# Program order on VectorE and ScalarE in the scan of an RWKV-7 / short-convolution layer

## The chip, the core and the metric

The kernel runs on one core of a Trainium2 chip. A core has five engines with a queue of instructions each: TensorE (PE; its weight loads are shown as PEld), VectorE (DVE), ScalarE (ACT), GpSimd (POOL) and SyncE (SP). SyncE only issues transfers here; nearly all of them go through its queue, and the few that store an inverse go through POOL's. The metric is the device time of one execution in microseconds (us), the median of several runs.

## What is computed

One layer for 128 context tokens and 2048 latent tokens of width 1024. The eight heads of group A go through RWKV-7, one scan per direction; group B is a gated short convolution; both go through one output projection.

```python
def step(S, inp):
    r_t, w_t, k_t, v_t, kk_t, a_t = inp
    s_kk = jnp.einsum('bdhij,bdhj->bdhi', S, kk_t)
    S = (S * w_t[..., None, :] - s_kk[..., :, None] * (kk_t * a_t)[..., None, :]
         + v_t[..., :, None] * k_t[..., None, :])
    return S, jnp.einsum('bdhij,bdhj->bdhi', S, r_t)
s_final, ys = lax.scan(step, s0.astype(f32), xs)
y = ys[:, 0] + jnp.flip(ys[:, 1], axis=1)
...
y = ((y - mean) * lax.rsqrt(var + GN_EPS)).reshape(b, t, A_WIDTH)
y = y * lp['gn_w'].astype(f32) + lp['gn_b'].astype(f32)
...
u = jnp.concatenate([ya, yb], axis=-1) @ lp['w_out']
return x + gate * u, s_final
```

Both token groups end in an RMS norm; the final states of the context scan are returned as well.

## The kernel before

Phase 1 (lines 50 to 596) makes the normalised input, all input projections, the scan's operands (`scr_ops`, per chunk of 64 tokens), the values (`scr_vt`), the convolution's result (`scr_mixT`) and the gates, and leaves them in DRAM. The change doesn't touch it.

Phase 2 is the scan. It goes through 17 tiles of 128 tokens (`NST`), in both directions at once; a tile has two chunks. `main()` is the loop over the steps s. The names that the text uses:

- `load_units` (L692) loads the operands kb and x of one step and direction, three steps ahead (`L(d)` in the loop).
- `cross` (L708, `C(k)`) makes, for a chunk and direction of step s + 2, the products of its operands (psG). ScalarE copies a part of them to lab, VectorE masks the others to abr and x, and lab is stored to `scr_at` (L728). There are four crosses in a step, C(0) to C(3), and a `turn` (`R(k)`, psT to kbt) behind each.
- `inverse` (L744) loads lab back in another layout (ab, L749), inverts sixteen pairs of triangular blocks on POOL (L758 to L769) and stores them to `scr_zt` (L774). It is issued behind C(3), for step s + 2.
- `merge` (L825) loads the inverse (zb, L829), transposes it on VectorE (L833), and puts two halves together with two groups of small matmuls, psU and psW, and ScalarE's copies (L841, L848). It has three parts. Parts one and two of merge s + 1 run at the end of step s, part three inside step s + 1, behind the first two parts of its `step`.
- `step` (L865) is the scan itself for one chunk of both directions: psw, psy, pst, psu, with copies on ScalarE (L894, L907) and a multiplication on VectorE (L919) between. sv is the state with the next values, loaded at L863.
- `finish` (L962) normalises a finished tile y, in two parts (psv, its root and reciprocal; then psr and the products L988 to L990).
- `project` (L1014) multiplies a tile with the output weights, in pieces of six matmuls (psoc for the convolution's half, psoa for attention's). It needs the tile mr or y split in two parts, mh (ScalarE, L1010) and ml (VectorE, L1011), and a tile z, to which VectorE adds the result (L1030, L1031). `piece()` runs one piece; a step has eight. The weights of the half are split by `load_k` (L996), first for the convolution, and at step 9 for attention.

Two things set the order. A scheduler puts the instructions of each engine, and the transfers of SyncE's queue, in the order in which they come ready in its own plan of the program, and then adds the waits. `Queue` (L638) overrules it for one engine: while `held` is set, each instruction depends on the one traced before it, so that the engine keeps the order of the program. Before the change only TensorE is such a queue in phase 2.

The PSUM pools of the scan have one buffer for each tag: g (two banks, a cross), t (one bank: turn, merge, finish), w, y and s (one each: step), and two of u (projections), eight banks in all.

Of the kernel before, what the change touches and what calls it, by code (L numbers as in the profile page):

```python
# [6 lines left out]
F32 = mybir.dt.float32  # L7
# [649 lines left out]
def phase2(K):  # L657
    nc, tc, A, S = K.nc, K.tc, K.A, K.S
    G = nc.gpsimd
    V, P, T = nc.vector, nc.scalar, Queue(tc, nc.tensor)  # L660
# [47 lines left out]
    def cross(s, i, d):  # L708

        un = units[s, i, d]  # L710
        pg = O.pg.tile([128, 2, 4, 2, 64], F32, tag="g", name=f"psG{s}{i}{d}")
        pb, px = pg[:, 0], pg[:, 1]
# [17 lines left out]
        V.tensor_tensor(un.abr[:], pb[:, :, 1, :], B.mx[:, 0, 1].unsqueeze(1).broadcast_to((128, 4, 64)), ALU.mult)  # L730
        for h in range(2):
            q = HR[1 - h]
            V.tensor_tensor(un.x[q, h].rearrange("r a p t -> r p a t"), px[q], B.mx[q, d].unsqueeze(1).broadcast_to((64, 4, 2, 64)), ALU.mult)  # L733

# [90 lines left out]
    def merge(s):  # L825
# [10 lines left out]
        pu = O.pt.tile([128, 16, 32], F32, tag="t", name=f"psU{s}")  # L836
# [6 lines left out]
        pw = O.pt.tile([128, 16, 32], F32, tag="t", name=f"psW{s}")  # L843
# [118 lines left out]
    def finish(t, y):  # L962
# [11 lines left out]
        P.activation(w[:], y[:], AF.Square)  # L974
        pv = O.pt.tile([128, 4, 2], F32, tag="t", name=f"psv{t}")
# [15 lines left out]
        yield  # L991
# [4 lines left out]
    def load_k(ks):  # L996
        wk.clear()
        for n, k in enumerate(ks):
            raw = tl(O.w, [128, 1024], "z", 2)
            D(raw[:], A["wout"][k * 128:(k + 1) * 128, :])  # L1000
            hi, lo = [tl(O.w, [128, 1024], f"wo{a}{n}", 1, F32R) for a in "hl"]
            P.copy(hi[:], raw[:])
            V.tensor_tensor(lo[:], raw[:], hi[:].bitcast(F32), ALU.subtract)
            wk.append((hi, lo))
# [3 lines left out]
    def parts(x):  # L1008
        mh, ml = [tl(O.w, [128, 4, 128], f"m{a}", 2, F32R) for a in "hl"]
        P.copy(mh[:], x[:])  # L1010
        V.tensor_tensor(ml[:], x[:], mh[:].bitcast(F32), ALU.subtract)  # L1011
        return mh, ml

    def project(t, att, x, z):  # L1014

        mh, ml = x
# [3 lines left out]
        for n, cs in enumerate(HALF):  # L1020
            ps = O.pu.tile([128, 512], F32, tag="u", name=f"pso{'ca'[att]}{t}{n}")
            for k in range(4):
# [4 lines left out]
                if k == 1:  # L1027
                    yield
            o = tl(O.w, [128, 512], "o", 1)
# [20 lines left out]
    def main():  # L1050
        setup_rest()
        T.held = True
        load_k((4, 5, 6, 7))
        jobs = []
        waiting = []
        convs = list(range(17))

        def refill():
            while len(jobs) < 2:
                if convs:  # L1060
                    t = convs.pop(0)
                    x = tl(O.w, [128, 4, 128], "mr", 1)
                    D(x[:], S["mixT"][:, t * 128:t * 128 + 128].rearrange("(k p) t -> p k t", p=128))
                    src, att = A["x"], 0
                elif B.att and waiting:
                    t, x = waiting.pop(0)
                    src, att = S["z0"], 1
                else:
                    return
                z = tl(O.w, [128, 1024], "z", 2)  # L1070
                D(z[:], src[t * 128:t * 128 + 128, :])
                jobs.append(project(t, att, parts(x), z))

        def piece(n=1):
            while n and jobs:
                try:
                    next(jobs[0])
                    n -= 1
                except StopIteration:
                    jobs.pop(0)  # L1080
                    refill()

        B.att = False
        run = lambda gen: [None for _ in gen]
        run(merge(0))
        refill()
# [144 lines left out]
```

## Time and profile before

| what | us |
|---|---|
| median of three runs (1903.23 to 1914.22) | 1905.8 |
| the profiled execution | 1912.77 |
| its span, first to last instruction | 1911.0 |
| phase 1, to the first step of the scan, about | 1055 |
| TensorE busy over the span | 1622.5 (85%) |
| VectorE busy | 1053.6 (55%) |
| ScalarE busy | 641.4 (34%) |
| POOL busy | 583.3 (31%) |

The page gives busy times and shares; further views list the instructions of one engine in order of time (start, length, engine, line, operation, output and inputs, count, and in brackets the idle time before it and what ended it), the waits in total (who waited for whom), the chain of work that ended last, and busy times for chosen windows. A busy engine need not be what the time hangs on: in the scan the engines wait for one another.

### The profile page before, as it was taken

The page shows a single profiled execution, that of the slowest core. Times are in us where ns is not written, and L with a number is a line of the kernel's source. Part 1 is how long each engine was busy: PE and PEld are TensorE (multiplying, and loading weights), DVE is VectorE, ACT ScalarE, POOL GpSimd, SP SyncE. Part 2 cuts the span into 40 slices and gives each one's busy share as a digit, 9 for nine tenths or more (in the row PEclk, how much of TensorE's full clock was granted, in tenths as well). Part 3 has the DMA queues.
Part 4 walks back from the last instruction along what each step waited for, and adds up shares of the span by engine and source line. Part 5 has one row for each costly group of instructions (what it writes and reads, how often), then busy time and mean ns, then how long its engine had stood idle before and what let it go on. Part 6 is the DMA issues. An engine that isn't in the chain of part 4 may idle for free.

```text
span 1911.0 us, 40886 instructions
## 1 busy us (share of the span) xinstructions
PE 1622.5 (85%) x16646; PEld 1418.5 (74%) x16646; DVE 1053.6 (55%) x1883; ACT 641.4 (34%) x1284; POOL 583.3 (31%) x1096
## 2 busy tenths in 40 slices
PE   5999999999899999988997887777777757887776
PEld 2998899998899999887897666566555546665554
DVE  5988877446766454876332543333333335555546
ACT  4565544224443223544110322222222223332332
POOL 0122100002121001212064154555555555555600
PEclk8999999999999999999898897888888779988888
DMA  8899996648899344887975665555556554556433
GB/s 336 227 226 254 226 264 245 220 130 177 183 188 225 127 158 128 208 191 193 243 205 168 180 160 141 153 143 144 153 144 179 160 129 119 139 145 159 123 111 111
DMA packets 390125, 339.90 MB, mean 178 GB/s; under 512 B 284137, under 2 KB 335209, under 8 KB 375857
## 3 DMA queue, kind: packets, MB, share of 16 engines
q1 hardware_dynamic: 387760, 332.82, 64.4%
q0 software_dynamic: 2176, 4.46, 1.5%
q8 instruction: 131, 2.15, 0.5%
q14 instruction: 58, 0.47, 0.1%
HBM read 215.68 MB, written 121.52 MB: 176 GB/s over the span
## 4 chain that ended last, share of the span: by engine, by line
PE 37%; DMA 21%; POOL 16%; DVE 13%; issue 6%; SPq 4%; ACT 2%; DVEq 0%; POOLq 0%; ACTq 0%
POOL zt L769 8%; DMA scr_ops<-sp 6%; POOL ztmp L766 5%; DMA kb<-scr_ops 3%; DMA ab<-scr_at 3%; DMA scr_at<-lab 3%; PE psoa L648 2%; DMA w<-scr_wsp 2%; PE mmgb L159 2%; PE mmc L159 2%; PE mmgb L161 2%; PE mmgb L160 2%; PE mmb L161 2%; PE mmc L161 2%; PE mmc L160 2%
## 5 line engine op out<-in xcount | busy, mean ns | idle before, releaser
L769 POOL TENSOR_TENSOR zt<-zt,ztmp 128x30 f32<-128x30 f32 (+7 forms) x510 | 204.4, 401 | 40.0
L766 POOL TENSOR_TENSOR ztmp<-ab,zt 128x60 f32<-128x60 f32 (+7 forms) x255 | 140.7, 552 | 20.0
L648 PE MATMUL psoa<-woh,mh 128*128 128x512 f32 x136 | 64.1, 471 | 82.2 <-ACT mh L1010 82.2
L315 POOL TENSOR_TENSOR shk<-rawl 128x384 f32<-128x384 f32 (+1 forms) x24 | 26.0, 1082 | 317.4 <-ACT rawl L311 305.2
L648 PE MATMUL psoc<-woh,mh 128*128 128x512 f32 x136 | 65.2, 480 | 59.2 <-DVE o L1030 59.2
L758 POOL COPY dgp<-ab 128x16 f32<-128x16 f32 x17 | 4.1, 240 | 354.8 <-DMA ab<-scr_at 354.7
L833 DVE STREAM_TRANSPOSE ws<-zb 32x512 f32<-32x512 f32 x34 | 23.8, 701 | 154.0 <-DMA zb<-scr_zt 153.3
L730 DVE TENSOR_TENSOR abr<-psG,mx 128x256 f32<-128x256 f32 x68 | 28.9, 424 | 134.3 <-ACT lab L723 134.2
L648 PE MATMUL psG<-x,kb 64*64 64x128 f32 x2176 | 87.2, 292 | 11.6 <-issue 4.6
L648 PEld LDWEIGHTS psoa<-woh,mh 128*128 128x128 f32 x136 | 28.2, 208 | 92.6 <-ACT mh L1010 87.0
L733 DVE TENSOR_TENSOR x<-psG,mx 64x512 f32<-64x512 f32 x136 | 93.6, 689 | 1.8
L648 PEld LDWEIGHTS psG<-x,kb 64*64 64x64 f32 x2176 | 68.7, 143 | 22.0 <-issue 16.4
L648 PEld LDWEIGHTS psoc<-woh,mh 128*128 128x128 f32 x136 | 29.3, 215 | 70.5 <-DVE o L1030 62.2
L648 PE MATMUL psT<-idt,kb 128*128 128x128 f32 x272 | 48.3, 305 | 28.4 <-ACT zb L848 26.1
L159 PE MATMUL mmk<-h,w 128*128 128x384 f32 (+1 forms) x184 | 61.5, 334 | 9.2 <-DMA w<-scr_wsp 9.2
L159 PE MATMUL mmg<-h,w 128*128 128x384 f32 (+1 forms) x192 | 63.4, 330 | 5.3 <-ACT rawc L318 3.0
L159 PE MATMUL mmv<-h,w 128*128 128x384 f32 (+1 forms) x192 | 64.9, 338 | 3.5 <-ACT q1r L313 3.0
L159 PE MATMUL mmgb<-h,w 128*128 128x384 f32 (+1 forms) x192 | 64.0, 333 | 3.2 <-DMA w<-scr_wsp 3.2
L159 PE MATMUL mmc<-h,w 128*128 128x384 f32 (+1 forms) x192 | 64.1, 334 | 0.0
L161 PE MATMUL mmgb<-h,w 128*128 128x384 f32 (+1 forms) x192 | 63.8, 332 | 0.1
L160 PE MATMUL mmgb<-h,w 128*128 128x384 f32 (+1 forms) x192 | 63.7, 332 | 0.0
L648 PEld LDWEIGHTS psT<-idt,kb 128*128 128x128 f32 x272 | 32.6, 151 | 41.7 <-ACT zb L848 29.6
(298 smaller groups left out, 5175.5 us busy)
## 6 DMA issues: line engine op xcount, KB each, us to landing
w<-scr_wsp SPq DMA_DIRECT2D x68, 1024.0 KB, 7.7
scr_wsp<-w SPq DMA_DIRECT2D x34, 1024.0 KB, 6.1
wr<-in_win SPq DMA_DIRECT2D x34, 512.0 KB, 6.9
kb<-scr_ops SPq DMA_DIRECT2D x34, 512.0 KB, 5.0
x<-scr_ops SPq DMA_DIRECT2D x68, 256.0 KB, 6.4
scr_ops<-sp SPq DMA_DIRECT2D x80, 192.0 KB, 4.5
scr_ops<-sp SPq DMA_DIRECT2D x160, 96.0 KB, 5.1
ab<-scr_at SPq DMA_DIRECT2D x34, 256.0 KB, 4.2
```

The costliest lines, as they stand in the source:

```text
L159: T.matmul(ps[:, :n], w[:, 0, k], hh[:, 0, k, :n], start=k == 0, stop=False)
L160: T.matmul(ps[:, :n], w[:, 0, k], hh[:, 1, k, :n], start=False, stop=False)
L161: T.matmul(ps[:, :n], w[:, 1, k], hh[:, 0, k, :n], start=False, stop=k == 7)
L315: G.tensor_tensor(s[:, lo:n].rearrange("p (r c) -> p r c", c=64), rp[:, :R, 0:64], rp[:, :R, 2:66], ALU.add)
L648: r = f(*args, **kw)
L730: V.tensor_tensor(un.abr[:], pb[:, :, 1, :], B.mx[:, 0, 1].unsqueeze(1).broadcast_to((128, 4, 64)), ALU.mult)
L733: V.tensor_tensor(un.x[q, h].rearrange("r a p t -> r p a t"), px[q], B.mx[q, d].unsqueeze(1).broadcast_to((64, 4, 2, 64)), ALU.mult)
L758: G.tensor_copy(dg[:], ab[:].rearrange("p j i -> p (j i)")[:, 1:1024:66])
L766: G.tensor_tensor(tv, ab[:, j:j + 2, j + 2:32].unsqueeze(1).broadcast_to((128, kn, 2, n)), zt[:, :kn, j:j + 2].unsqueeze(3).broadcast_to(( ...
L769: G.tensor_tensor(zt[:, :kn, j + 2:32], zt[:, :kn, j + 2:32], tv[:, :, r], ALU.add)
L833: V.transpose(zr[r0], zb[r0, :, 0:32])
```

## The change

`Queue` now also wraps VectorE and ScalarE in phase 2, and `main()` sets `held` for all three. A held engine waits wherever the program has put a wait, so several places of the program move:

- A cross has a tile of one bank for each kind of product (tags b and x) instead of one tile of two banks, and x is masked before abr.
- Merge uses bank w, the one of `step`, instead of t. All three parts of merge s + 1 run at the end of step s, with pieces between.
- `finish` has four parts, and `F()` is called seven times a step.
- The next projection's tiles are loaded by `take()` while the present one runs; its mh is made before the third piece of the present one (`head`), its ml at the end (`split`). `project` yields before the second half is added.
- The weights are split by a generator; for attention it runs one part per piece in step 9.

```diff
-    V, P, T = nc.vector, nc.scalar, Queue(tc, nc.tensor)
+    V, P, T = Queue(tc, nc.vector), Queue(tc, nc.scalar), Queue(tc, nc.tensor)
...
-        pg = O.pg.tile([128, 2, 4, 2, 64], F32, tag="g", name=f"psG{s}{i}{d}")
-        pb, px = pg[:, 0], pg[:, 1]
+        pb = O.pg.tile([128, 4, 2, 64], F32, tag="b", name=f"psB{s}{i}{d}")
+        px = O.pg.tile([128, 4, 2, 64], F32, tag="x", name=f"psX{s}{i}{d}")
...
-        V.tensor_tensor(un.abr[:], pb[:, :, 1, :], B.mx[:, 0, 1].unsqueeze(1).broadcast_to((128, 4, 64)), ALU.mult)
         for h in range(2):
             q = HR[1 - h]
             V.tensor_tensor(un.x[q, h].rearrange("r a p t -> r p a t"), px[q], B.mx[q, d].unsqueeze(1).broadcast_to((64, 4, 2, 64)), ALU.mult)
+        V.tensor_tensor(un.abr[:], pb[:, :, 1, :], B.mx[:, 0, 1].unsqueeze(1).broadcast_to((128, 4, 64)), ALU.mult)
...
-        pu = O.pt.tile([128, 16, 32], F32, tag="t", name=f"psU{s}")
+        pu = O.q.tile([128, 16, 32], F32, tag="w", name=f"psU{s}")
...
-        pw = O.pt.tile([128, 16, 32], F32, tag="t", name=f"psW{s}")
+        pw = O.q.tile([128, 16, 32], F32, tag="w", name=f"psW{s}")
...
         P.activation(w[:], y[:], AF.Square)
+        yield 1
...
         V.reciprocal(r[:], r[:])
-        yield
+        yield 1
         rb = tl(O.l, [128, 8, 64], "fw", 1)
         P.copy(rb[:], r[:].unsqueeze(2).broadcast_to((128, 8, 64)))
+        yield 1
...
-    def load_k(ks):
+    def weights(ks):
+
         wk.clear()
+        raws = []
         for n, k in enumerate(ks):
...
+            raws.append(tl(O.w, [128, 1024], "z", 2))
+            D(raws[n][:], A["wout"][k * 128:(k + 1) * 128, :])
+            if n:
+                yield 1
+            for i in (range(n - 1, n + 1) if n == 3 else range(n - 1, n)):
+                if i >= 0:
+                    hi, lo = [tl(O.w, [128, 1024], f"wo{a}{i}", 1, F32R) for a in "hl"]
+                    P.copy(hi[:], raws[i][:])
+                    V.tensor_tensor(lo[:], raws[i][:], hi[:].bitcast(F32), ALU.subtract)
+                    wk.append((hi, lo))
+                    if i == 2:
+                        yield 1
...
+            if n:
+                yield
             o = tl(O.w, [128, 512], "o", 1)
...
-        T.held = True
-        load_k((4, 5, 6, 7))
...
+        for e in (T, V, P):
+            e.held = True
+        run = lambda gen: [None for _ in gen]
+        run(weights((4, 5, 6, 7)))
...
         def piece(n=1):
...
+            for _ in range(n):
+                if B.load:
+                    if next(B.load, 0) == 0:
+                        B.load = None
+                    continue
+                if not nxt:
+                    take()
+                if not now:
+                    if nxt:
+                        j = nxt.pop()
+                        split(j)
+                        now.append(j)
+                    continue
+                j = now[0]
+                if j.k == 2 and nxt:
+                    nxt[0].headed = True
+                    head(nxt[0])
+                next(j.run)
+                j.k += 1
+                if j.k == 4:
+                    run(j.run)
+                    now.clear()
+                    if nxt:
+                        m = nxt.pop()
+                        split(m, m.headed)
+                        now.append(m)
...
+        def F(n=1):
+
+            if fin:
+                t, y, f = fin[0]
+                if next(f, 0) == 0:
+                    fin.pop(0)
+                    waiting.append((t, y))
+                    if fin:
+                        next(fin[0][2])
...
             if s == 9:
-                while jobs or convs:
+                while now or nxt or convs:
                     piece()
-                load_k((0, 1, 2, 3))
                 B.att = True
-                refill()
+                B.load = weights((0, 1, 2, 3))
+            while len(before) > 1 and before[-2] in held:
+                piece()
...
             next(a), next(a)
-            next(m, None)
+            F()
             C(0)
             R(0)
             next(a)
+            F()
             C(1)
             R(1)
             next(a), next(a)
-            finish_a(0)
+            F()
             C(2)
             piece()
             R(2)
             L(0)
+            F()
             a = step(s, 1)
             next(a), next(a)
-            finish_a(1)
             C(3)
             if u:
                 inverse(u)
             R(3)
             L(1)
+            F()
             next(a)
             piece()
-            finish_b()
+            F()
             piece()
             next(a), next(a)
+            F()
+            piece(2)
+            m = merge(s + 1) if s + 1 < NST else iter(())
+            next(m, 0), next(m, 0)
+            piece(2)
+            next(m, 0)
             piece()
-            finish_b()
-            piece()
-            if s + 1 < NST:
-                m = merges[s + 1] = merge(s + 1)
-                next(m), next(m)
-            piece(3)
```

`take()` issues the loads of the next projection's mr (or takes a finished y) and z; `head(j)` is the copy to mh, `split(j)` the subtraction to ml, with the copy ahead of it where it hasn't been made.

More of the change, by code (lines that the diff above doesn't have):

```diff
@@ new lines, in head, with split @@
+        def head(j):
+            j.mh = tl(O.w, [128, 4, 128], "mh", 2, F32R)
+            P.copy(j.mh[:], j.x[:])
+        def split(j, half=False):
+            if not half:
+                head(j)
+            j.ml = tl(O.w, [128, 4, 128], "ml", 2, F32R)
+            V.tensor_tensor(j.ml[:], j.x[:], j.mh[:].bitcast(F32), ALU.subtract)
+            if j.att:
+                held.discard(j.t)
+        B.load = None
+        held = set()
+        fin = []
+        def F(n=1):
[6 more added lines that the diff above has]
+                        next(fin[0][2])
```

83 lines of the change are left out of this document (26 added, 57 removed).

## The prediction

> **What bounds the kernel now.** I read the page first (span, shares, the chain that ended last), then the table of waits from 1055 us on, where the scan runs, then the order of one scan step on SyncE's queue. The chain of the scan is not TensorE's: it returns every step to POOL and to transfers.
>
> ```profile
> span 1911.0 us, 40886 instructions
> ...
> PE 37%; DMA 21%; POOL 16%; DVE 13%; issue 6%; SPq 4%; ACT 2%; DVEq 0%; POOLq 0%; ACTq 0%
> ```
>
> ```profile
> POOL dgp L758 <- DMA ab<-scr_at: 296.7, 15, 60.8
> DVE ws L833 <- DMA zb<-scr_zt: 153.3, 15, 15.4
> ...
> PE psoa L648 <- ACT mh L1010: 82.2, 15, 20.1
> ...
> PE psoc L648 <- DVE o L1030: 59.2, 7, 10.0
> ```
>
> Columns: who waited for what, total us, times, longest. VectorE stands 153.3 us at the merge's transposes (L833) until zb has come, and what is queued behind them there (o and z of a projection, y of a finished tile) keeps TensorE: 59.2 and 82.2 us. These are the waits that the change can take away. But POOL itself stands 296.7 us waiting for ab. Why, SyncE's queue says (start us, length, what):
>
> ```profile
> 1321.63 0.38 SPq L829 DMA_DIRECT2D zb<-scr_zt  x1
> 1322.06 3.05 SPq L728 DMA_DIRECT2D scr_at<-lab  x4
> ...
> 1325.70 2.54 SPq L701 DMA_DIRECT2D x<-scr_ops  x4
> 1328.34 2.36 SPq L728 DMA_DIRECT2D scr_at<-lab  x4
> ...
> 1335.88 1.12 SPq L749 DMA_DIRECT2D ab<-scr_at  x2
> ...
> 1372.22 0.38 SPq L829 DMA_DIRECT2D zb<-scr_zt  x1
> ```
>
> ```profile
> SPq L829 <- DMA scr_zt<-zt: 223.1, 21, 19.7
> ```
>
> ```profile
> 1360.14 1.04 PE L648 MATMUL psG<-x,kb 64*64 64x128 f32 x28
> ```
>
> The scheduler has put the load of zb (for merge s+1, L829) ahead of the stores of lab (L728) that inverse s+2 needs. SyncE stands at zb until the inverse before has landed (223.1 us in all). The last cross product of the next step is done at 1361.2, yet its lab is stored only after the zb load of 1372.22. So the inverses run one after the other with two transfers between them, and the cycle closes without TensorE. From the chain of waits of the same step:
>
> ```profile
> 1330.40 5.29 DMA scr_at<-lab
> ...
> 1336.41 4.92 DMA ab<-scr_at
> ...
> 1341.48 0.22 POOL dgp L758
> ...
> 1367.86 1.96 POOL scr_zt L774 x3
> ```
>
> Cycle: 1321.6 to 1330.4 on SyncE's queue 8.8; store 5.3 and ab 4.9 with their issues to 1341.5, 11.1; POOL to 1367.9, 26.4; the store of zt to 1372.2, 4.3: 50.6 us.
>
> ```profile
> 1123.21 0.38 SPq L829 DMA_DIRECT2D zb<-scr_zt  x1
> ...
> 1819.94 0.37 SPq L829 DMA_DIRECT2D zb<-scr_zt  x1
> ```
>
> Fifteen such loads from first to last make 14 cycles, 49.8 us each on the mean.
>
> ```profile
> 1322.00:1372.00 50.00, 36.86 (x648) 29.36 (x648) 17.92 (x28) 12.07 (x24) 25.49 (x56) 0.83 0.57 149
> ```
>
> In one (busy us of PE, PEld, DVE, ACT, POOL) TensorE works 36.9 of 50: 13 us in which it may wait for anything.
>
> **The change part by part.** No instruction or transfer is added or dropped; order and banks move.
>
> *Hold on VectorE and ScalarE.* L833 now stands behind all that precedes merge s+1 in the program. The 59.2 and 82.2 us go, but the next thing late is psU of that merge, which needs the same zb at the same time. Inside the 14 cycles I cost it at nothing: the cover is the cycle on SyncE and POOL, whose queues are not held. Bounds per cycle: below, the order of SyncE's queue as it once came out better; above, as it came out worse.
>
> ```profile
> 1511.33 2.97 SPq L701 DMA_DIRECT2D x<-scr_ops  x4
> 1520.69 0.39 SPq L829 DMA_DIRECT2D zb<-scr_zt  x1
> ...
> 1563.13 0.38 SPq L829 DMA_DIRECT2D zb<-scr_zt  x1
> ...
> 1567.20 2.03 SPq L728 DMA_DIRECT2D scr_at<-lab  x4
> ...
> 1611.32 0.37 SPq L829 DMA_DIRECT2D zb<-scr_zt  x1
> 1611.79 2.71 SPq L863 DMA_DIRECT2D sv<-scr_vt  x2
> ...
> 1664.83 0.37 SPq L829 DMA_DIRECT2D zb<-scr_zt  x1
> ```
>
> With x ahead of zb a cycle was 42.4 us (1520.69 to 1563.13), with the sv loads behind zb too it was 53.5. Three late cycles are of the long kind. Normalisation in four steps takes its chain of small waits out of TensorE's line in just these steps, so I let the sv loads come first there again: 3 times 2.7, minus 8 us (bounds 0 and minus 8).
>
> *Start.* The eight splits of the weights now stand ahead of merge 0 on both engines.
>
> ```profile
> 1054.54 0.45 PE L648 MATMUL psw<-sv,x 128*64 128x64 f32 x2 [12.07 <-DMA sv<-scr_vt]
> ...
> 1064.35 1.10 PE L648 MATMUL psG<-x,kb 64*64 64x128 f32 x32 [1.86 <-ACT sv L907]
> ...
> 1077.84 1.10 PE L648 MATMUL psG<-x,kb 64*64 64x128 f32 x32 [2.22 <-DVE x L733]
> ```
>
> ```profile
> 1036.23 0.69 DVE L833 STREAM_TRANSPOSE ws<-zb 32x512 f32<-32x512 f32 x1
> ...
> 1059.44 2.48 DVE L1003 TENSOR_TENSOR wol<-z,woh 128x1024 fp32r<-128x1024 f32 x2 [3.55 <-ACT woh L1002]
> ```
>
> ```profile
> 1042.51 1.16 ACT L848 COPY zb<-psW 32x512 f32<-32x512 f32 x2 [2.02 <-PE psW L648]
> ```
>
> Merge 0, from its first transpose to its last copy 7.4 us (1036.2 to 1043.7), was done while sv was awaited; now it begins when the last split ends, 1061.9, and the first psw, which shares its bank, follows at 1069.3 instead of 1054.5, 15 later. The two waits for ScalarE and VectorE, 1.9 and 2.2, arose while these engines also split weights, and go: plus 11 us on the first inverse (bounds 0, if the weights load sooner, and 15).
>
> *Cross products.* Two tiles for one of two banks; x before abr. abr waited for lab as both read one bank, and x followed; now x runs beside lab. TensorE waited for x 2.2 us in the whole scan (the row of 1077.84): at most that, counted above. lab alone leads to the inverse.
>
> *Merge.* Bank w instead of t: turn no longer waits for zb's copies. psW moves before the next step, whose psw must now wait for two copies (1.2 us, the row of 1042.51); a piece of six matmuls stands between. Zero while a cycle has 13 us spare; up to 1.2 a step otherwise.
>
> *Projections.* Loads of mr and z are issued one projection ahead, and projections now end after pieces 1 and 5 of a step's eight, not 4 and 8. So a store of z and a load of mr (0.5 us each on SyncE's queue) may come between zb and the lab stores: bounds 0 and plus 1 a cycle; I take 0, where mr stood behind ab. A held head (mh) that waits for mr has lab's copies behind it on ScalarE; as the cross products end 11 us before zb (1361.2 against 1372.2), that is hidden up to 11 us. The weights for attention are split piecewise in step 9, which lies in a cycle of normal length: zero.
>
> *Tail.* After the last zb there is no inverse left.
>
> ```profile
> 1825.23 1.42 DVE L833 STREAM_TRANSPOSE ws<-zb 32x512 f32<-32x512 f32 x2 [8.81 <-DMA zb<-scr_zt]
> ```
>
> ```profile
> 1829.93 0.80 PE L648 MATMUL psoa<-woh,mh 128*128 128x512 f32 x1 [12.39 <-ACT mh L1010]
> ...
> 1839.48 1.20 PE L648 MATMUL psU<-ws,lab 32*32 32x32 f32 x64 [0.71 <-DVE y L988]
> ```
>
> TensorE stands 12.4 us for mh, whose y is behind L833. Held, this work (1829.9 to 1839.5) is done before zb comes, and psU can follow the transposes at 1826.7 instead of 1839.5: minus 13 us (bounds 0, if the end then waits for the last projections, and minus 16, the idle time left in the last 53 us).
>
> *Sum.* Plus 11, minus 8, minus 13: minus 10. The profiled execution took 1912.8 (its span 1911.0 and 1.8 around it), 7.0 above the median of 1905.8. So 1902.8 for such an execution, and **1896 us** for the median.
>
> [...]
>
> ```profile
> 1341.00:1368.00 27.00, 22.56 (x50) 0.87 0.37 123
> ...
> 1785.00:1815.00 30.00, 26.06 (x49) 0.93 0.36 120
> ```
>
> (us, then POOL's busy time.) The same instructions of an inverse keep POOL 22.6 us busy in one step and 26.1 in a late one, where attention projections and normalisation give VectorE more to do beside it. If VectorE no longer stands before zb, more of its work falls beside the inverse; half that difference, 1.75, in the ten early cycles is plus 18 us. [...]
>
> **The rivals.**
> *A, forecast (0.45).* SyncE's order stays; start, late cycles and tail give 1896; own range 1872 to 1920.
> *B, shorter cycles (0.21).* The new plan puts zb behind kb and x, as before 1563: 14 cycles at 42.4 are minus 104 instead of minus 8: about 1800. For it: zb and the lab stores lie within a few us of each other in the plan, so little flips them. Against it, psoa's busy time in a step:
>
> ```profile
> 1521.00:1563.00 42.00, 1.00 (x5) 0.47 (x3) 0.68 (x1) 0.85 0.44 114
> ```
>
> The step with 5 projection matmuls of the usual 48 or so still ends with zb (1563.13) ahead of the last lab stores (1567.20).
> *C, slower (0.17).* Held engines stall in the plan, which moves zb ahead of the sv loads in the eleven other cycles as well: 2.7 each, plus 30, and the minus 8 is lost: 1896 + 38, about 1934. It decides once the planned step grows by some 2 us.
> *D, POOL slowed (0.12).* Plus 18: 1914.
> *E, no effect (0.05).* The order was nearly the program's: 1906. Against it: L833 ahead of y.
>
> **How the numbers follow.** A measurement of this kernel tells about 0.5% from no change: below 1896.3 is faster, above 1915.3 slower. A lies on the bound: 0.22 faster, 0.17 same, 0.06 slower. B 0.21 faster; C 0.17 slower; D 0.09 same, 0.03 slower; E 0.05 same. Faster 0.43, same 0.31, slower 0.26. The range runs from B's time less 10 to C's plus 6, which leaves out a B with zb behind ab and a C with the cost of the mr loads.
>
> **What would show it.** The distance of zb loads (49 us: A; 42: B; over 52: C); what follows zb on SyncE's queue; POOL's wait for ab, 20 us a step if A holds; POOL's busy time in an inverse (D); the first psw (1069), psU after the last zb (7 us). Wrong would be an inverse that starts before the zb load of its step, or TensorE without waits at psU.

## The result: 4% slower, and where the time lies

The changed kernel takes 1984.9 us (median; 1981.2 to 1989.8), the kernel before beside it 1908.4: a ratio of 1.040, interval 1.036 to 1.044. The forecast was 1896 us with a range up to 1940.

First the page of the changed kernel, its span and the busy times of the engines:

```profile
span 1984.5 us, 40833 instructions
...
PE 1646.4 (83%) x16646; PEld 1439.3 (73%) x16646; DVE 1052.3 (53%) x1883; ACT 641.0 (32%) x1284; POOL 585.6 (30%) x1096
```

VectorE and POOL have no more to do than before (1052.3 us, before 1053.6; 585.6, before 583.3). TensorE has the same 16646 matmuls and takes 23.9 us longer for them (before 1622.5), at a mean granted clock of 0.899 over the span (before 0.918; more in the last section). The other 50 of the 73.5 us that the span gained, TensorE waits. The table of waits of the same kernel, from 1055 us on (who waited for whom, total us, times, longest):

```profile
POOL dgp L758 <- DMA ab<-scr_at: 329.2, 15, 75.4
...
PE psU L648 <- DVE ws L648: 172.9, 34, 35.7
...
DVE o L648 <- PE psoa L648: 109.3, 25, 6.9
DVE o L648 <- PE psoc L648: 98.2, 25, 7.4
...
PE psoa L648 <- DVE ml L648: 49.4, 12, 14.8
...
DVE ws L648 <- DMA zb<-scr_zt: 26.6, 5, 7.4
...
PE psoa L648 <- ACT mh L648: 20.9, 9, 3.3
```

Every instruction of the three held engines has line 648 now (the helper's), so the names of the tiles tell them apart. Before, VectorE stood 153.3 us at the transposes until zb came. Now it waits for zb itself in five of the merges only (26.6 us, all between zb(5) and zb(9)); in the others zb has been there for long when VectorE reaches the transposes. TensorE stands at psU until they are made: 172.9 us, before 15.6. VectorE itself stands 207.5 us at o, the sum behind a projection's matmuls (before 61.5), and the transposes stand behind it in its order.

The longest single wait at psU has another thing in front, the splits of the attention weights in step 9 (ScalarE, VectorE and TensorE, in order of time):

```profile
1546.88 1.04 ACT L648 CAST woh<-z 128x1024 fp32r<-128x1024 f32 x1 [31.26 <-DMA z<-in_wout]
1547.96 1.22 DVE L648 TENSOR_TENSOR wol<-z,woh 128x1024 fp32r<-128x1024 f32 x1 [28.68 <-ACT woh L648]
...
1551.60 0.28 PE L648 MATMUL psU<-ws,lab 32*32 32x32 f32 x2 [35.73 <-DVE ws L648]
```

zb was asked for at 1524.32, but its transposes stand behind splits that wait for the weights' load, which SyncE issued only at 1540.69, behind zb, the lab stores and ab. Merge 0 has a wait of the same kind (26.6 us).

The loads of zb cut the scan into stretches; the rows of zb(2), zb(5), zb(10), of one late load and of the last, on SyncE's queue (start, length):

```profile
1138.71 0.36 SPq L829 DMA_DIRECT2D zb<-scr_zt  x1
...
1301.81 0.37 SPq L829 DMA_DIRECT2D zb<-scr_zt  x1
...
1524.32 0.37 SPq L829 DMA_DIRECT2D zb<-scr_zt  x1
...
1698.10 0.37 SPq L829 DMA_DIRECT2D zb<-scr_zt  x1
...
1868.68 0.37 SPq L829 DMA_DIRECT2D zb<-scr_zt  x1
```

Worked out from such rows of each kernel, in us of one profiled execution (zb(n) is the load for merge n; e1 and e2 are the first two experiments):

| kernel | to zb(2) | zb(2) to (5) | (5) to (10) | (10) to (16) | zb(16) to end | span |
|---|---|---|---|---|---|---|
| before | 1123.2 | 148.9 | 248.6 | 299.2 | 91.1 | 1911.0 |
| before, engines held (e2) | 1134.2 | 158.1 | 250.7 | 320.5 | 134.3 | 1997.9 |
| changed, engines not held (e1) | 1120.9 | 142.7 | 223.0 | 323.0 | 85.2 | 1894.6 |
| changed | 1138.7 | 163.1 | 222.5 | 344.4 | 115.8 | 1984.5 |

The change is two changes. The hold alone costs 11, 9, 2, 21 and 43 us in the five stretches, 86.9 in all; the moved parts alone give 2, 6 and 26, take 24, and give 6: 16.4 gained. Both together would be +70.5; +73.5 was measured. The totals agree better than the stretches do (at the end 43 less 6 would be 37, and it is 25), for the hold keeps another order of the program in e2 than in the changed kernel.

The stretches are cut where SyncE issues zb, on the side of POOL. TensorE comes to psU of the same merge 5 to 39 us later, and 912 matmuls are recorded behind the last load of zb in the changed kernel, 680 before. Cut at the first matmul of psU instead, the change loses 19, 6, 0, 35 and 13 us. So the last columns of these tables share out between late cycles and end what depends on the cut; their sum does not.

What the hold does in a late cycle is shown by the chain of waits of the changed kernel (start, length, what):

```profile
1720.61 4.63 DMA out_y<-z
1725.26 3.51 DMA z<-scr_z
1728.82 0.69 DVE o L648
...
1730.23 0.61 DVE ws L648
1730.87 0.71 DVE ws L648
1731.63 1.91 PE psU L648 x62
```

The zb of this merge had been asked for at 1698.10. Its transposes start at 1730.23, because a projection's sum stands ahead of them in VectorE's order, and that sum waits for a tile z, whose buffer was only free once an earlier result had landed in DRAM. Before, POOL's work fills much of the chain of the late cycles (its lines L766 and L769 have 29% of it from 1521 to 1820); from 1576 on the changed kernel's chain has none of it. What closes these cycles now is TensorE's matmuls, VectorE's order, and the transfers of lab, z and out_y between them.

TensorE stands little at psU in these last cycles, as it comes late itself. Two rows of its waits from zb(11) to zb(16), 1576.9 to 1868.7:

```profile
PE psoa L648 <- DVE ml L648: 42.6, 10, 14.8
...
PE psU L648 <- DVE ws L648: 14.3, 10, 2.7
```

It is the next projection that waits there, for ml, which stands behind the norm of the one before.

The end shows VectorE's order at length, its rows after the last zb (1868.68; in brackets the idle time and what ended it):

```profile
1888.30 0.69 DVE L648 TENSOR_TENSOR o<-psoa,gl 128x512 f32<-128x512 f32 x1 [3.47 <-PE psoa L648]
...
1894.18 0.68 DVE L648 TENSOR_TENSOR o<-psoa,gl 128x512 f32<-128x512 f32 x1
1894.90 0.69 DVE L648 TENSOR_TENSOR z<-z,o 128x512 f32<-128x512 f32 x1
1896.44 0.16 DVE L648 TENSOR_TENSOR ss<-ss 128x1 f32<-128x1 f32 x1 [0.85 <-ACT o L648]
1896.96 0.16 DVE L648 RECIPROCAL ss<-ss 128x1 f32<-128x1 f32 x1 [0.36 <-ACT ss L648]
1897.16 1.29 DVE L648 SCALAR_TENSOR_TENSOR z<-z,ss,fg 128x1024 f32<-128x1024 f32 x1
1898.36 0.69 DVE L648 TENSOR_TENSOR ml<-y,mh 128x512 fp32r<-128x512 f32 x1
1898.96 1.43 DVE L648 STREAM_TRANSPOSE ws<-zb 32x512 f32<-32x512 f32 x2
```

The sums, the norm with two turns over ScalarE, its product and the next ml all come first: psU starts at 1899.80, 31.1 us after the load of zb was issued. Before it was 19.5 (1819.94 to 1839.48).

### The profile page after: what moved, and what is told of

Its sections match the earlier page's. It is cut to its first block, busy times and chain, and to the rows that moved or that the text cites. A ratio compares the mean times of both kernels' runs of the same rounds, so it can differ in the third digit from the quotient of the medians.

```text
span 1984.5 us, 40833 instructions
## 1 busy us (share of the span) xinstructions
PE 1646.4 (83%) x16646; PEld 1439.3 (73%) x16646; DVE 1052.3 (53%) x1883; ACT 641.0 (32%) x1284; POOL 585.6 (30%) x1096
## 5 line engine op out<-in xcount | busy, mean ns | idle before, releaser
L769 POOL TENSOR_TENSOR zt<-zt,ztmp 128x30 f32<-128x30 f32 (+7 forms) x510 | 210.4, 412 | 40.0
L648 PE MATMUL psU<-ws,lab 32*32 32x32 f32 x1088 | 37.3, 237 | 172.9 <-DVE ws L648 172.9
L648 DVE TENSOR_TENSOR x<-psX,mx 64x512 f32<-64x512 f32 x136 | 93.6, 688 | 150.6 <-PE psB L648 127.7
L648 PEld LDWEIGHTS psU<-ws,lab 32*32 32x32 f32 x1088 | 33.2, 150 | 181.3 <-issue 172.9
L766 POOL TENSOR_TENSOR ztmp<-ab,zt 128x60 f32<-128x60 f32 (+7 forms) x255 | 137.9, 541 | 20.0
L648 PE MATMUL psoa<-woh,ml 128*128 128x512 f32 x136 | 67.2, 494 | 49.4 <-DVE ml L648 49.4
L648 PE MATMUL psX<-x,kb 64*64 64x128 f32 x1088 | 84.2, 285 | 0.0
L648 PEld LDWEIGHTS psB<-x,kb 64*64 64x64 f32 x1088 | 62.7, 137 | 23.1 <-issue 17.5
L648 PEld LDWEIGHTS psoa<-woh,ml 128*128 128x128 f32 x136 | 32.3, 237 | 64.1 <-DVE ml L648 56.8
L648 PE MATMUL psB<-x,kb 64*64 64x128 f32 x1088 | 74.7, 277 | 3.0 <-DVE abr L648 1.7
L159 PE MATMUL mmv<-h,w 128*128 128x384 f32 (+1 forms) x192 | 66.6, 347 | 2.7 <-ACT q1r L313 1.5
L159 PE MATMUL mmgb<-h,w 128*128 128x384 f32 (+1 forms) x192 | 63.7, 332 | 1.5 <-DMA w<-scr_wsp 1.5
L160 PE MATMUL mmv<-h,w 128*128 128x384 f32 (+1 forms) x192 | 64.8, 337 | 0.0
```

The costliest lines, as they stand in the source:

```text
L159: T.matmul(ps[:, :n], w[:, 0, k], hh[:, 0, k, :n], start=k == 0, stop=False)
L160: T.matmul(ps[:, :n], w[:, 0, k], hh[:, 1, k, :n], start=False, stop=False)
L648: r = f(*args, **kw)
L766: G.tensor_tensor(tv, ab[:, j:j + 2, j + 2:32].unsqueeze(1).broadcast_to((128, kn, 2, n)), zt[:, :kn, j:j + 2].unsqueeze(3).broadcast_to(( ...
L769: G.tensor_tensor(zt[:, :kn, j + 2:32], zt[:, :kn, j + 2:32], tv[:, :, r], ALU.add)
```

## The experiments

**All results** (us; ratio to the kernel before beside it, with its interval; then the stretches of the table above):

| run | median | ratio | to zb(2) | 2–5 | 5–10 | 10–16 | end |
|---|---|---|---|---|---|---|---|
| e1_loose_vp | 1898.6 | 0.994 [0.991, 0.996] | 1120.9 | 142.7 | 223.0 | 323.0 | 85.2 |
| e2_before_held | 1999.9 | 1.048 [1.043, 1.053] | 1134.2 | 158.1 | 250.7 | 320.5 | 134.3 |
| e3_release9 | 1935.7 | 1.013 [1.009, 1.017] | 1140.2 | 165.0 | 225.6 | 323.6 | 82.9 |
| e4_hold_v | 1992.9 | 1.043 [1.039, 1.047] | 1139.0 | 167.1 | 230.7 | 339.9 | 118.5 |
| e8_merge_free | 1938.1 | 1.014 [1.010, 1.018] | 1125.7 | 156.8 | 220.5 | 330.6 | 104.2 |
| e9_proj_free | 1913.4 | 1.001 [0.999, 1.004] | 1146.9 | 147.6 | 212.5 | 328.6 | 84.6 |
| e12_merge0_first | 1974.3 | 1.034 [1.030, 1.037] | 1122.9 | 158.5 | 227.4 | 346.9 | 114.0 |
| e13_transpose_early | 1965.3 | 1.029 [1.025, 1.032] | 1134.5 | 154.5 | 225.5 | 333.9 | 115.0 |
| e14_sums_free | 1957.0 | 1.025 [1.021, 1.029] | 1134.7 | 146.0 | 212.5 | 342.3 | 118.0 |
| e15_norm_free | 1939.8 | 1.014 [1.012, 1.017] | 1141.6 | 163.1 | 220.3 | 327.7 | 84.4 |
| e19_split_first | 1952.1 | 1.021 [1.017, 1.025] | 1144.2 | 159.9 | 223.0 | 328.4 | 94.6 |
| e6_off_after | 2009.1 | 1.053 [1.047, 1.059] | 1141.8 | 162.4 | 217.9 | 369.2 | 119.2 |
| e7_off_loose | 1907.4 | 0.999 [0.996, 1.001] | 1127.5 | 143.9 | 218.5 | 338.1 | 84.8 |
| e10_zb_last | 1890.4 | 0.989 [0.986, 0.992] | 1137.1 | 142.9 | 235.8 | 286.4 | 86.1 |
| e11_zb_last_before | 1869.4 | 0.978 [0.975, 0.981] | 1137.7 | 132.9 | 220.3 | 289.6 | 89.0 |
| e16_proj_free_zb_last | 1880.9 | 0.986 [0.982, 0.990] | 1160.3 | 137.6 | 224.6 | 281.2 | 87.2 |
| e17_after_zb_last | 1968.1 | 1.029 [1.027, 1.031] | 1150.1 | 142.4 | 233.7 | 322.7 | 118.3 |
| e18_zb_pool | 1877.7 | 0.982 [0.979, 0.985] | 1123.7 | 137.3 | 235.0 | 291.4 | 94.5 |

(Where zb is put behind ab, its load is issued later in a cycle, so the first column can't be set against the others. The stretches are of the profiled execution; for e9 and e16 it was 9 and 12 us above the median.)

### Is it the hold, or what was moved?

e1, the changed kernel:

```diff
-        for e in (T, V, P):
-            e.held = True
+        T.held = True
```

> The changed kernel with only TensorE held, as before the change; all moved parts and banks stay. Theory H (the hold costs: VectorE and ScalarE in program order put a projection's sum and split ahead of the merge and of the crosses' copies): the 73 us go, 1890 to 1930. Theory M (the moved parts cost: three merge parts in a row, weights ahead of merge 0, loads one projection ahead): stays above 1960.

e2, the kernel before, with the first line of the change and `held` set for all three engines:

```diff
-    V, P, T = nc.vector, nc.scalar, Queue(tc, nc.tensor)
+    V, P, T = Queue(tc, nc.vector), Queue(tc, nc.scalar), Queue(tc, nc.tensor)
...
-        T.held = True
+        for e in (T, V, P):
+            e.held = True
```

> The kernel before with VectorE and ScalarE held too, and nothing moved. Theory H: clearly slower than before, 1960 or more, since the program there gives the held engines no better place for the merge. Theory M: within 1% of before, 1890 to 1930.

e3, the changed kernel, released in step 9:

```diff
             if s == 9:
...
+                for e in (V, P):
+                    e.held = False
                 B.att = True
```

> The changed kernel with VectorE and ScalarE released at step 9, when the attention projections begin. Theory H with its place in the attention steps (late cycles +45, end +25, middle cycles -26): 1985 - 70 = 1915 (1895 to 1935), with zb loads 49 to 50 us apart from zb(10) on. If the hold costs in all steps alike: about 1950. Theory M: 1985.

e4, the changed kernel with `for e in (T, V)` in `main()`.

> The changed kernel with TensorE and VectorE held, ScalarE released. If VectorE's order carries the loss (transposes and masks behind z's sum): 1970 to 1990. If ScalarE's does (lab and zr copies behind mh and the squares): under 1930. If each needs the other: between.

Measured 1898.6, 1999.9, 1935.7 and 1992.9. The hold costs the time (theory H): taking it away gives 86 us, adding it to the old program costs 88. VectorE's hold alone is enough, and ScalarE's adds nothing to it (ScalarE held without VectorE was not run). e3 came out just above its first case and missed its cycles: they went to 54 (323.6 / 6), not to 49 or 50. So half of the 45 us in the late cycles doesn't come from the hold, and e1 has the same 323.0.

### What stands ahead of what in VectorE's order?

e8, merge's transposes and copies go past the hold; e9, a projection's sums, squares and norm do (in each line `V.` becomes `nc.vector.`, `P.` becomes `nc.scalar.`):

```diff
-            V.transpose(zr[r0], zb[r0, :, 0:32])
+            nc.vector.transpose(zr[r0], zb[r0, :, 0:32])
...
-            V.tensor_tensor(o[:], ps[:], g[:, cs], ALU.mult)
-            V.tensor_tensor(z[:, cs], z[:, cs], o[:], ALU.add)
+            nc.vector.tensor_tensor(o[:], ps[:], g[:, cs], ALU.mult)
+            nc.vector.tensor_tensor(z[:, cs], z[:, cs], o[:], ALU.add)
```

> The changed kernel, in which only the merge's instructions on VectorE and ScalarE (transposes, copies behind psU and psW) are not held; all others keep the program's order. Theory S (the transposes stand behind a projection's sum, norm and ml, so psU comes late): late cycles (after it 57.4 on the mean, released 54) and end go back, and merge 0 no longer waits for the weights' splits: 1985 - 21 - 30 - 15 = 1919 (1900 to 1940). Rival X (the crosses' copies and masks or the scan's own copies stand behind held work instead): 1970 or more.

> The changed kernel, in which only a projection's sums, squares and norm are not held (splits mh and ml, merge, crosses and normalisation keep the order). Theory S: what stands ahead of the transposes is gone but for ml: late cycles and end go back, the start doesn't: 1985 - 21 - 30 = 1934 (1920 to 1950). Rival X: 1970 or more. If ml and y in front of the transposes matter more than the sums: about 1960.

e9 takes the whole loss away: 1913.4, level with the kernel before, though merge, crosses and normalisation are still held and the start is as late as ever. That is more than expected, so the sums and the norm hold up more than the transposes; e8, with merge alone released, gives 47 us, at the upper edge of its first case.

e14 and e15 split e9: e14 releases only the two lines of o and z above, e15 only the squares, root, reciprocal and last product.

> The changed kernel in which only o and z (a projection's sums on VectorE) are not held; squares, root, reciprocal and the last product stay in order. Theory O (VectorE waits there for TensorE, 98 us at psoc and 109 at psoa, and the transposes behind it): most of the 71 us that releasing the whole epilogue gave: 1985 - 50 to 70 = 1915 to 1935. Rival N (the norm's turn over ScalarE and the store and load of z behind it): 1965 or more.

> The changed kernel in which only the norm (squares and root on ScalarE, sum, reciprocal and last product on VectorE) is not held. Theory O: it exists only in the attention steps and is short: 1985 - 0 to 20 = 1965 to 1985. Rival N: 1985 - 45 or more, under 1940, all of it behind zb(10).

Theory O fell for the late part. The sums are worth 31 us of span (1984.5 against 1953.5), nearly all of it before zb(10): 17 and 10 in the two early stretches, 2 in the late one and nothing at the end. The norm is worth 47 (1937.1): 17 in the late cycles and 31 at the end, nothing before. (Cut at psU, the sums' share stays before merge 10, and the norm's is 35 and 12.) By medians they are worth 28 and 45 us; e9, both at once, gave 71.5, so the two prices add up.

The splits of the weights in step 9 are still held in these runs: psU of that merge starts 26 to 28 us after the load of zb in e9, e14, e15 and e19, as in the changed kernel (27.3), and 5.9 and 5.7 after it in e3 and e8, where the transposes don't stand behind them (before 5.7). No run releases these splits alone, so their price stays open.

e19 moves one split, everything held:

```diff
                 if j.k == 4:
-                    run(j.run)
                     now.clear()
                     if nxt:
                         m = nxt.pop()
                         split(m, m.headed)
                         now.append(m)
+                    run(j.run)
```

> The changed kernel, all held, with the split of the next projection (ml) traced ahead of the last sum and norm of the present one, not behind them. If the norm costs by standing ahead of ml, for which the next psoa waits: the end goes back by 20 to 30 and the late cycles by 10 to 20: 1985 - 40 = 1945 (1930 to 1960). If it costs by standing ahead of the transposes: no more than 10 of it, 1975 or more.

1952.1; late cycles 16 less, end 21 less, as the first case said. In the waits of e19 no psoa stands at ml any more (49.4 us before this edit). So e19 gains, by order alone, 37 of the 48 us that e15 gains in the late cycles and at the end: most of the norm's price there is its place ahead of ml. (e19 puts ml ahead of the last sum too, but the sums cost nothing there, e14.) But psU's wait, from the tables of waits of e19 and of e9:

```profile
PE psU L648 <- DVE ws L648: 226.1, 34, 37.8
```

```profile
PE psU L648 <- DVE ws L648: 203.1, 34, 27.4
```

It is longer than the 172.9 of the changed kernel, in kernels that are 33 and 71 us faster. TensorE comes sooner to the same place. In six merges of e19 and seven of e9 VectorE waits there for zb itself (42.2 and 51.8 us in all); in the others its own order still ends the wait, 11 to 34 us after zb was asked for. The total of one wait is no price.

e13 places the transposes two pieces sooner, e12 merge 0 ahead of the weights:

```diff
+            m = merge(s + 1) if s + 1 < NST else iter(())
+            next(m, 0)
             piece(2)
-            m = merge(s + 1) if s + 1 < NST else iter(())
-            next(m, 0), next(m, 0)
+            next(m, 0)
...
+        run(merge(0))
         run(weights((4, 5, 6, 7)))
...
-        run(merge(0))
```

(the first three edits are e13's, the last two e12's)

> The changed kernel with the merge's transposes traced two pieces sooner (psU stays where it is). Theory S: VectorE no longer has to end two pieces' sums, waiting for TensorE, before TensorE gets its transposes: of the 173 us at psU a half or more goes: 1985 - 30 to 60 = 1925 to 1955. Rival: in the early and middle cycles zb lands later than that place, and the sums wait behind it: 1980 to 2000.

> The changed kernel with merge 0 traced ahead of the weights' splits. If the splits ahead of merge 0 cost the start (first zb of the scan 15.5 later) and nothing more: 1970. If the three cycles behind it (+14) are late for the same reason: 1955. If the start is late for another held wait: 1985.

e13 gave 20 us, less than hoped: VectorE then waits for zb itself (81.1 us in all, 26.6 without the edit). e12 gave 15.8 us at zb(2) and 10.6 of the median: the start is the weights' splits ahead of merge 0, and not much more.

### SyncE's order, on which the forecast rested

e6 and e7 take the lab stores and ab loads out of SyncE's queue, in the changed kernel and in e1:

```diff
-                D(S["at"][s, b, d * 8:d * 8 + 8, h].rearrange("u j i -> j u i"), x)
+                P.dma_start(S["at"][s, b, d * 8:d * 8 + 8, h].rearrange("u j i -> j u i"), x)
...
-            D(ab[h * 64:h * 64 + 64].rearrange("p j i -> p (j i)"), at.rearrange("b u h j i -> (b u h) (j i)"))
+            G.dma_start(ab[h * 64:h * 64 + 64].rearrange("p j i -> p (j i)"), at.rearrange("b u h j i -> (b u h) (j i)"))
```

> The changed kernel with the stores of lab issued by ScalarE and the loads of ab by POOL, so that SyncE's order no longer stands between a cross and its inverse. Theory S (in the late steps the held VectorE and TensorE, not SyncE, close the cycle): late cycles stay at 54 or more, end stays near 116; middle cycles may fall by 0 to 4 each: 1960 to 1985. Rival Q (the hold only made SyncE's order worse): the cycles go under 48 everywhere, 1850 to 1900.

> The same transfers moved off SyncE in the changed kernel with only TensorE held (1898.6). If SyncE's order closes the cycle there (zb and the loads of sg ahead of lab's stores), cycles fall to POOL's 26.4 and 4.3 and the transfers' 10, 41 to 45: 14 times 6 less, about 1815 (1790 to 1840). If TensorE does: 1880 to 1900.

Neither did what was expected: e6 is slower than the changed kernel, and e7's late cycles went from 54 to 56. The timeline of e7, ScalarE with the loads that SyncE issued meanwhile:

```profile
1652.43 0.37 ACT L648 COPY lab<-psB 128x256 f32<-128x256 f32 x1 [0.61 <-PE psB L648]
1656.94 0.37 SPq L829 DMA_DIRECT2D zb<-scr_zt  x1
...
1663.75 0.45 SPq L968 DMA_DIRECT2D mr<-scr_q  x1
...
1664.91 4.09 ACTq L648 DMA_DIRECT2D scr_at<-lab  x4
...
1669.04 0.59 ACT L648 COPY kbt<-psT 128x512 f32<-128x512 f32 x1 [16.24 <-DMA mr<-scr_q]
```

lab was ready at 1652.8, its stores were issued from 1664.9 on, behind zb and the loads after it on SyncE, and ScalarE did nothing else for 16 us. The trace's records say why. All transfers of the two queues count on the same eight semaphores (counters of finished transfers), numbers 101 to 103 and 105 to 109, and each waits for the last one that used its own. The first of these four stores has 108, that of the load of kb at 1659.66; the last has 103, that of the load of mr at 1663.75. So the stores were still tied to SyncE's queue, and the two runs don't decide between their theories.

e10 (in e1) and e11 (in the kernel before) leave the queue and add one edge:

```diff
-            D(ab[h * 64:h * 64 + 64].rearrange("p j i -> p (j i)"), at.rearrange("b u h j i -> (b u h) (j i)"))
+            K.ab = D(ab[h * 64:h * 64 + 64].rearrange("p j i -> p (j i)"), at.rearrange("b u h j i -> (b u h) (j i)")).ins
...
-        D(zb[:], S["zt"][s % 3].rearrange("u h r c -> (h r) u c"))
+        r = D(zb[:], S["zt"][s % 3].rearrange("u h r c -> (h r) u c"))
+        tc.add_manual_dep(r.ins, K.ab.name, mybir.DependencyInfo(mybir.DependencyClass.NoSync, mybir.DependencyReason.DATA), reason="order")
```

> The changed kernel with only TensorE held (1898.6), and each load of zb put behind the ab loads issued ahead of it in the program, so that lab's stores and ab no longer stand behind zb on SyncE. Theory Q (SyncE's order closes the cycles that are still long, 54 each from zb(10) on; the middle ones, 44.6, are TensorE's own): late cycles go to 44 to 48, middle ones stay: 1898 - 48 = 1850 (1830 to 1870). Rival T (TensorE and VectorE close the late cycles even unheld): 1885 to 1900.

> The kernel before with the same one edge (zb behind ab). Theory Q: all 14 cycles of 49.8 go to what TensorE takes, 44 to 46: 1908 - 14 times 5 = 1838 (1820 to 1860). Rival T: within 1% of before, since psU then waits for a later zb.

e11, one edge in the kernel before, is the fastest of all: 1869.4, 2.2% less than before. Its middle cycles are 44.1 (220.3 / 5; before 49.7). A step's chain of waits in it:

```profile
1396.15 4.98 DMA scr_at<-lab
...
1401.80 0.61 SPq L749
...
1402.59 5.97 DMA zb<-scr_zt
1408.59 0.71 DVE ws L834
...
1410.08 1.91 PE psU L648 x62
1411.98 6.71 PE psoc L648 x18
```

POOL is not in this stretch of it: lab's store goes out first, zb follows ab at once, and then TensorE's own work closes the cycle. e11 stayed 31 us above its 1838: zb now waits for ab, and the late cycles are still 48. In e10 the late cycles fell as theory Q said (53.8 to 47.7), while the middle ones rose from 44.6 to 47.2; by its time alone it would be rival T's.

e17 is the same edge in the changed kernel, e16 in e9; e18 has zb loaded by POOL in the kernel before (`G.dma_start` for `D` in `merge`).

> The changed kernel, held, with each zb load put behind the ab loads on SyncE. If the held VectorE and TensorE close the cycles, SyncE's order is cover for nothing: within 1% of 1985, 1965 to 1995. If SyncE's order is part of the loss: 1985 - 30 or more, under 1955.

> The changed kernel with the projections' epilogue released (1913) and zb behind the ab loads on SyncE. If the rest of the hold costs nothing: as the unheld kernel with that edge, 1890 (1880 to 1900). If held transposes and copies still cost: over 1900. If the hold itself gains something: under 1869, the kernel before with the same edge.

> The kernel before with zb loaded by POOL (right behind the stores of zt, ahead of the next inverse), so that no transfer on SyncE waits for an inverse and zb doesn't wait for ab. If the cycle of 49.8 is SyncE's order and TensorE's own is 43 to 44: 14 times 6 and no waiting at psU behind a late zb: 1908 - 84 = 1825 (1810 to 1850). If TensorE with VectorE and ScalarE closes the cycle at 44 and 53 as with zb behind ab: 1860 to 1875. If POOL's wait for its own stores ahead of each inverse counts: 14 times 3 more, 1880 to 1910.

With the engines held the same edge gives 17 us (1968.1) and leaves the end at 118: SyncE's order is a small part of what the held kernel loses. e16 at 1880.9 lies in its first case: what is left of the hold costs nothing there, and gains nothing that e11 hasn't. e18 at 1877.7 lies between two of its own: better than zb ahead of lab's stores, no better than zb behind ab. No held kernel beats e11.

## Why the prediction was wrong, step by step

**What bounds the kernel: right.** zb ahead of the lab stores on SyncE, and the inverse behind it, closed the cycle of 49.8 us. One edge against that order (e11) took 5.7 us off each middle cycle.

**"Inside the 14 cycles I cost it at nothing": this step failed.** The cover was said to be the cycle on SyncE and POOL, "whose queues are not held". It covers VectorE only while VectorE reaches the transposes before zb lands. The step said that the waits of 59.2 and 82.2 us go and that the next thing late needs the same zb at the same time. The waits of psoc at o and of psoa at mh mostly went (psoa now stands 49.4 us at ml instead), but in ten of the fifteen merges psU was late behind VectorE's own order, not with zb. The prediction named what stood behind the transposes before, and never listed what would stand ahead of them: o, which waits for the matmuls just issued, the norm with its turns over ScalarE, and ml. Runs e9, e14 and e15 give that list its prices: sums 31 us, norm 47. Put at nothing, the hold costs 33 us in the 14 cycles in the old program (e2 against before) and 41 in the new one (the changed kernel against e1). Of the cases, none fits the spacing of the loads of zb throughout: they are 54.4, 44.5 and 57.4 us apart in the three stretches.

**The weights in step 9, "zero": failed too.** VectorE waits 28.7 us there for a split with the transposes behind it, and TensorE 35.7 at psU. From psU to psU that cycle took 65.7 us, the four before it 44.7. What this costs in the end was not tried alone.

**Tail, minus 13: failed with the hold, right in kind without it.** In e1 psU follows zb as forecast; its rows (PE, then VectorE's transposes):

```profile
1814.71 0.24 PE L648 MATMUL psU<-ws,lab 32*32 32x32 f32 x2 [4.82 <-DVE ws L648]
```

```profile
1813.96 1.43 DVE L648 STREAM_TRANSPOSE ws<-zb 32x512 f32<-32x512 f32 x2 [12.09 <-DMA zb<-scr_zt]
```

zb was issued at 1809.42: 5.3 us, forecast 7. But the end gained 6 us of the 13 even there, and held it is 25 us longer than before (13 from psU on). "Held, this work is done before zb comes" was the mistake: the projection's work isn't done, as it waits on TensorE and ScalarE in turn.

**Start, plus 11: right mechanism, at its bound.** The first psw came at 1069.75 (forecast 1069), zb(2) 15.5 us later (bounds 0 and 15), and e12 took back 15.8. The 4 us that two waits were to give back did not show.

**Cross products, at most 2.2: right in kind.** abr waited for lab 56 times before (108.9 us in all) and once in the changed kernel (3.9), where x, now ahead of abr, runs beside lab (they start at 1420.04 and 1419.99 in one cross). TensorE waits 1.7 us for abr at psB instead of 2.2 for x.

**Late cycles, minus 8: failed.** The sv loads still stand behind zb. SyncE's waits in the changed kernel:

```profile
SPq L863 <- PE psy L648: 130.0, 14, 19.9
```

They wait for psy of a late TensorE (40.5 us before). Besides, the moved parts alone lengthen these cycles by 24 us (e1). In e1's queue the loads of sg, q and y stand between zb and the last lab stores (zb at 1702.28, ab at 1720.82: 18.5 us; 15.2 in the kernel before, 1664.83 to 1680.03). With zb behind ab the late cycles of the new program are no longer than those of the old (286.4 and 289.6), so SyncE's order holds these 24 us; that it is these loads was not tried alone.

**Held head mh, "hidden up to 11 us": nothing contradicts it.** ScalarE's hold adds nothing (e4 against the change).

**The rivals.** B came true in part, for another reason: the middle cycles, from one load of zb to the next, fell from 49.7 to 44.5, by the moved parts and not by the hold (44.6 in e1, 50.1 in e2). One such cycle on SyncE's queue in the changed kernel:

```profile
1420.48 2.47 SPq L728 DMA_DIRECT2D scr_at<-lab  x4
...
1434.86 0.37 SPq L829 DMA_DIRECT2D zb<-scr_zt  x1
1435.28 3.68 SPq L728 DMA_DIRECT2D scr_at<-lab  x4
...
1441.01 1.12 SPq L749 DMA_DIRECT2D ab<-scr_at  x2
```

Half of the lab stores now go ahead of zb. C had the right sign and the wrong cause (3 us a cycle for sv; the end alone cost 25). D fell. Windows of before and of the change, the early and middle cycles first, where D put its 18 us, then the late ones (us of window; PE, PEld, DVE, ACT, POOL busy; granted clock):

```profile
1123.00:1521.00 398.00, 298.95 (x5229) 238.86 (x5228) 148.43 (x231) 98.70 (x192) 208.88 (x449) 0.83 0.59 155
```

```profile
1139.00:1524.00 385.00, 281.20 (x5148) 226.34 (x5148) 142.54 (x223) 97.19 (x190) 210.49 (x448) 0.85 0.58 155
```

```profile
1521.00:1820.00 299.00, 217.97 (x3777) 171.23 (x3775) 154.46 (x278) 95.44 (x201) 167.45 (x336) 0.87 0.52 136
```

```profile
1524.00:1869.00 345.00, 235.05 (x3568) 183.48 (x3568) 149.13 (x267) 91.11 (x191) 169.35 (x336) 0.78 0.49 130
```

POOL is busy 210.5 us instead of 208.9 in the first pair and 169.4 instead of 167.5 in the second. D's 3.5 us were too large as well: over these windows of before an inverse takes POOL 26.1 us early (208.9 / 8) and 27.9 late (167.5 / 6). That VectorE's work beside an inverse lengthens it, from which D had its 1.75 us a cycle, no run shows: with 142.5 us of VectorE in the early and middle window of the changed kernel POOL takes 1.6 us more than with the 148.4 of before, and late, with 149.1 against 154.5, 1.9 more.

**The number without the hold.** e1, the changed kernel with only TensorE held, takes 1898.6 us, 3 from the forecast of 1896. That is luck: forecast were plus 11, minus 8 and minus 13 at the start, late and at the end; e1 has minus 2 at the start, minus 32 in the early and middle cycles, plus 24 in the late ones and minus 6 at the end.

**Chances.** The rival that ended on the slower side was a transfer a few us late. One in which a held engine waits, with work behind it that TensorE needs, was not among the cases, and the range ended 45 us too low for that reason.

## What to carry to other kernels

Before an engine is held to the program's order, write down for each instruction that TensorE waits for what stands ahead of it on that engine, and what that in turn waits for; a sum or a norm that waits for the matmuls just issued is better placed behind the transposes and splits that the next matmuls need, and so is a split that waits for a load. A total of waits at one place shows where to look, not what there is to gain; releasing one group of instructions from the order, one run each, gives the price. And where a plan has put a load that waits ahead of stores that are ready, one ordering edge in that queue can be worth more than a change of the whole program.

## What the runs showed of the hardware

TensorE's long waits had slow matmuls behind them. After the 6 us wait at the last psU of the changed kernel, matmuls of one size, TensorE's rows:

```profile
1899.80 0.28 PE L648 MATMUL psU<-ws,lab 32*32 32x32 f32 x2 [6.03 <-DVE ws L648]
...
1902.88 0.63 PE L648 MATMUL psoa<-wol,mh 128*128 128x512 f32 x1
...
1905.49 0.39 PE L648 MATMUL psoa<-woh,ml 128*128 128x512 f32 x1
```

0.63 us each, and 0.39 from 5 us after the wait on. The granted clock is 1.00 until 1898.2 us, 4.4 us after the last matmul ahead of the wait (1893.8), 0.50 from there to 1905, and 1.00 from 1905 to 1908. In the kernel before, the six matmuls of psoa behind the wait of 12.4 us for mh (1817.6 to 1829.9) took 0.80 and five times 0.63 us, at a granted clock of 0.50 from 1821 to 1833; the next six, from 1835.3 on, took 0.50 and five times 0.39 to 0.40, at 1.00. In the two late windows above the granted clock fell from 0.87 to 0.78. Over the whole program the same 408 matmuls of psoa took 201.4 us, before 181.8. So the stall of VectorE's order at the last psU cost its own 6 us and the slow matmuls behind it.

The other surprise is e7: there the lab stores, moved to ScalarE's queue, were not free of SyncE's, as the program had the two queues share counters. ScalarE's stores waited 12.1 us from the end of lab (1652.8) for loads with which they have no data in common.
